# Fewer, larger store packets in a batch-norm + ReLU kernel, and five rows computed in two parts

## Chip, cores, metric

One NeuronCore of one Trainium2 chip. The metric is device time in microseconds (us) of one execution; lower is better. A ratio is the mean time of one kernel's fast runs over that of the kernel before in the same rounds, so not quite the ratio of the medians beside it. Runs of one batch share a chip.

## The reference

```python
# x: (32, 128, 32, 32) float32; one scale and one bias per channel
normalized = (x - running_mean[None, :, None, None]) / np.sqrt(running_var[None, :, None, None] + eps)
scaled = normalized * gamma[None, :, None, None] + beta[None, :, None, None]
return np.maximum(scaled, 0).astype(np.float32)
```

16.78 MB are read and 16.78 MB are written. Each element needs one multiply, one add and one maximum, which ScalarE (ACT) does in a single activation (128 x 1024 elements in 1.227 us on average, 30 of them in the kernel before).

## The kernel before

Each of the 128 partitions holds 16 whole images ("rows" of 1024 floats, 4 KB) of each half of the batch; in DRAM those 16 rows are contiguous. So a DMA of n rows is one run of n x 4 KB per partition. Loads are issued from SyncE, stores from ScalarE after the activations of their rows.

```python
J = 16
TILES = ((0, 0, 2), (0, 2, 4), (0, 4, 8), (0, 8, 16), (1, 0, 16))   # (half, first row, end)
LOAD_CUTS = {(1, 8)}
STORE_CUTS = {(0, 1)}
HALVES = {(0, 0), (0, 1)}          # rows whose activation is done in two parts
...
    for t, a, b in TILES:
        xt = data.tile([P, b - a, HW], F32, name=f"x{t}_{a}")
        cuts = [a] + [j for j in range(a + 1, b) if (t, j) in LOAD_CUTS] + [b]
        for c, d in zip(cuts, cuts[1:]):
            nc.sync.dma_start(out=xt[:, c - a : d - a, :], in_=xr[t, :, c:d, :])
...
        for t, a, b, xt in tiles:
            first = a
            for j in range(a, b):
                step = HW // 2 if (t, j) in HALVES else HW
                for w in range(0, HW, step):
                    nc.scalar.activation(out=xt[:, j - a, w : w + step], in_=xt[:, j - a, w : w + step],
                        func=ACTF.Relu, bias=bias_t[:, j : j + 1], scale=scale_t[:, j : j + 1])
                if j + 1 == b or (t, j + 1) in STORE_CUTS:
                    nc.scalar.dma_start(out=outr[t, :, first : j + 1, :], in_=xt[:, first - a : j + 1 - a, :])
                    first = j + 1
```

The cut parts are the views, the pools, and the parameters (four loads of 0.5 KB, a small matmul that spreads them over the partitions, five small instructions for scale and bias).

## Time and profile before

| | |
|---|---|
| time | 83.92 us, median of 3 (83.75 to 83.99) |
| span in the profile, from first to last instruction | 82.0 us |
| ScalarE busy | 39.1 us |
| loads, bytes per partition's run | 8, 8, 16, 32, 32, 32 KB |
| stores, bytes per partition's run | 4, 4, 8, 16, 32, 64 KB |

This profile is read from the bytes: loads and stores take 48.7% + 47.6% of the 16 DMA engines' span. The lines are in the prediction.

### The profile page before, as it was taken

The numbers are of one execution on the slowest core, as the hardware profiler recorded it, in microseconds if no ns is written. First come the engines' busy times: TensorE is split into PE (matmuls) and PEld (weight loads), VectorE is DVE, ScalarE is ACT, GpSimd is POOL, SyncE is SP. The second block draws the span as 40 slices with busy tenths as digits, with TensorE's granted clock in tenths as the row PEclk, the third lists the DMA queues.
The fourth block names the chain that finished last, engine by engine and source line by source line (L and its number), as shares of the span: only waits on it lengthen the run. The fifth ranks groups of instructions, "written<-read, shape, count | busy, mean of one in ns | idle before, by whom it ended". The sixth has DMA issues, their size and how long they took to land.

```text
span 82.0 us, 120 instructions
## 1 busy us (share of the span) xinstructions
PE 0.7 (1%) x2; PEld 0.5 (1%) x2; DVE 0.8 (1%) x5; ACT 39.1 (48%) x36; POOL 0.8 (1%) x6
## 2 busy tenths in 40 slices
PE   0002000000000000000000000000000000000000
PEld 0002000000000000000000000000000000000000
DVE  0000300000000000000000000000000000000000
ACT  0600477799239999199994199993000000000000
POOL 3000000000000000000000000000000000000000
DMA  2899997979899989999799799998992999996590
GB/s 48 336 424 456 416 544 336 524 322 526 338 434 430 506 358 506 390 434 444 320 460 500 316 424 448 512 432 368 480 736 128 416 512 512 512 512 288 224 512 0
DMA packets 1792, 33.56 MB, mean 409 GB/s; under 512 B 256, under 2 KB 256, under 8 KB 512
## 3 DMA queue, kind: packets, MB, share of 16 engines
q1 hardware_dynamic: 864, 16.78, 48.7%
q10 hardware_dynamic: 928, 16.78, 47.6%
HBM read 16.78 MB, written 16.78 MB: 409 GB/s over the span
## 4 chain that ended last, share of the span: by engine, by line
DMA 56%; ACT 10%; issue 2%; SPq 0%
DMA x<-in_x_dram 56%; ACT x L102 10%; SPq L56 0%
## 5 line engine op out<-in xcount | busy, mean ns | idle before, releaser
L102 ACT ACTIVATE x<-x,bias_t,scale_t 128x1024 f32<-128x1024 f32 (+1 forms) x34 | 37.5, 1177 | 9.9 <-DMA x<-in_x_dram 7.6
L86 ACT ACT_TABLE_LOAD x1 | 1.3, 1283 | 2.6 <-issue 2.6
L86 ACT ACTIVATE std_t<-cols,eps_t 128x16 f32<-128x16 f32 x1 | 0.3, 273 | 4.5 <-PE cols L78 4.5
L78 PE MATMUL cols<-raw,rep 8*128 8x64 f32 x2 | 0.7, 429 | 7.6 <-DMA raw<-in_beta_dram 7.6
L78 PEld LDWEIGHTS cols<-raw,rep 8*128 8x128 f32 x2 | 0.5, 306 | 7.6 <-issue 7.6
L68 POOL TENSOR_SCALAR_AFFINE_SELECT rep<-rep 8x128 f32<-8x128 f32 x1 | 0.4, 392 | 0.1
L88 DVE RECIPROCAL rstd_t<-std_t 128x16 f32<-128x16 f32 x1 | 0.3, 254 | 7.7 <-ACT std_t L86 7.7
L67 POOL MEMSET rep<- 8x128 f32 x1 | 0.2, 194 | 0.3 <-POOLq L130 0.3
L90 DVE TENSOR_TENSOR scale_t<-cols,rstd_t 128x16 f32<-128x16 f32 x1 | 0.2, 175 | 0.1
L92 DVE TENSOR_TENSOR ms_t<-cols,scale_t 128x16 f32<-128x16 f32 x1 | 0.2, 175 | 0.0
L94 DVE TENSOR_TENSOR bias_t<-cols,ms_t 128x16 f32<-128x16 f32 x1 | 0.2, 174 | 0.0
L130 POOL MEMSET const-bfloat16-1.0<- 128x1 bf16 x1 | 0.1, 106 | 0.0
L130 POOL MEMSET const-uint8-127<- 128x1 uint8 x1 | 0.1, 106 | 0.0
L130 POOL MEMSET const-float32-0.0<- 128x1 f32 x1 | 0.1, 103 | 0.3 <-issue 0.3
L130 POOL MEMSET const-float32-1.0<- 128x1 f32 x1 | 0.1, 103 | 0.0
L65 DVE MEMSET eps_t<- 128x1 f32 x1 | 0.1, 59 | 0.9 <-PEq L130 0.9
## 6 DMA issues: line engine op xcount, KB each, us to landing
x<-in_x_dram SPq DMA_DIRECT2D x3, 4096.0 KB, 38.7
out_dram<-x ACTq DMA_DIRECT2D x1, 4096.0 KB, 28.7
x<-in_x_dram SPq DMA_DIRECT2D x2, 1024.0 KB, 5.8
x<-in_x_dram SPq DMA_DIRECT2D x1, 2048.0 KB, 11.3
out_dram<-x ACTq DMA_DIRECT2D x1, 2048.0 KB
out_dram<-x ACTq DMA_DIRECT2D x2, 512.0 KB, 19.6
out_dram<-x ACTq DMA_DIRECT2D x1, 1024.0 KB
raw<-in_running_var_dram ACTq DMA_DIRECT2D x1, 0.5 KB
```

The source lines that it names most:

```text
L65: nc.vector.memset(eps_t, float(eps))
L67: nc.gpsimd.memset(rep, 1.0)
L68: nc.gpsimd.affine_select(out=rep, in_=rep, compare_op=mybir.AluOpType.is_equal, fill=0.0, base=0, pattern=[[0, P // Q], [-1, Q]], channel ...
L78: nc.tensor.matmul(cols.rearrange("p k j -> p (k j)"), rep.rearrange("q r s -> q (r s)"), raw.rearrange("q k j -> q (k j)"), start=True, s ...
L86: nc.scalar.activation(out=std_t, in_=cols[:, 0, :], func=ACTF.Sqrt, bias=eps_t[:, 0:1], scale=1.0)
L88: nc.vector.reciprocal(out=rstd_t, in_=std_t)
L90: nc.vector.tensor_mul(out=scale_t, in0=cols[:, 1, :], in1=rstd_t)
L92: nc.vector.tensor_mul(out=ms_t, in0=cols[:, 2, :], in1=scale_t)
L94: nc.vector.tensor_sub(out=bias_t, in0=cols[:, 3, :], in1=ms_t)
L102: nc.scalar.activation(out=xt[:, j - a, w : w + step], in_=xt[:, j - a, w : w + step], func=ACTF.Relu, bias=bias_t[:, j : j + 1], scale=sc ...
L130: nc = _bacc.Bacc("TRN2", target_bir_lowering=False, num_devices=1)
```

## The change

The intent: one store fewer (packets of 4, 12, 16, 32 and 64 KB), rows 0 to 3 in one tile, and five rows rather than two computed in two parts.

```diff
-TILES = ((0, 0, 2), (0, 2, 4), (0, 4, 8), (0, 8, 16), (1, 0, 16))
+TILES = ((0, 0, 4), (0, 4, 8), (0, 8, 16), (1, 0, 16))

-LOAD_CUTS = {(1, 8)}
+LOAD_CUTS = {(0, 2), (1, 8)}
 STORE_CUTS = {(0, 1)}

-HALVES = {(0, 0), (0, 1)}
+HALVES = {(0, 0), (0, 1), (0, 2), (0, 3), (0, 4)}
```

## The prediction

> **What bounds the kernel now.** I read the page first: its span, its busy row for the DMA engines and its list of queues.
>
> ```profile
> span 82.0 us, 120 instructions
> ...
> PE 0.7 (1%) x2; PEld 0.5 (1%) x2; DVE 0.8 (1%) x5; ACT 39.1 (48%) x36; POOL 0.8 (1%) x6
> ...
> DMA packets 1792, 33.56 MB, mean 409 GB/s; under 512 B 256, under 2 KB 256, under 8 KB 512
> ...
> q1 hardware_dynamic: 864, 16.78, 48.7%
> q10 hardware_dynamic: 928, 16.78, 47.6%
> ```
>
> The two DMA queues, q1 for the loads and q10 for the stores, take 48.7% + 47.6% = 96.3% of what 16 engines have in the span. ScalarE (ACT), the one engine with real work, is busy for less than half of it. The bytes are fixed: 16.78 MB in, 16.78 MB out. The packet count tells the packet's form: 864 is 6 loads x (128 + 16), so each partition's run is one packet, however long, and each DMA has 16 small packets more (4 bytes, its completion signal, one for each engine). So "2 rows" means an 8 KB packet and "16 rows" a 64 KB one.
>
> Next the packet records of the trace, which give start, duration and size of each. A data packet takes 0.159 us for 4 KB, 0.309 for 8 KB, 0.611 for 16 KB, 1.213 for 32 KB and 2.418 for 64 KB; load and store packets of one size take the same, and 16 engines at 32 KB in 1.213 us move 432 GB/s. The first packet starts at 1.75 us, the last ends at 80.81. All durations together are 1263.9 us, or 78.99 us for each of 16 engines, in a stretch of 79.06 us. Summed by whole microseconds, the share is 1.00 to 1.02 in every one from 3 to 79. So the engines never stand empty, and the time is the sum of the packets, plus 1.75 us ahead of them and 1.2 us after.
>
> Then the timeline and the chain of waits, for what stands just behind this bound. Columns of the timeline: start, duration, engine, work.
>
> ```profile
> 9.61 1.52 ACT L102 ACTIVATE x<-x,bias_t,scale_t 128x512 f32<-128x512 f32 x2 [1.02 <-DVE bias_t L94]
> 11.16 0.37 ACTq L110 DMA_DIRECT2D out_dram<-x  x1
> 11.58 1.52 ACT L102 ACTIVATE x<-x,bias_t,scale_t 128x512 f32<-128x512 f32 x2 [0.45 <-ACT x L102]
> 13.13 0.37 ACTq L110 DMA_DIRECT2D out_dram<-x  x1
> 13.55 2.37 ACT L102 ACTIVATE x<-x,bias_t,scale_t 128x1024 f32<-128x1024 f32 x2 [0.45 <-ACT x L102]
> 15.95 0.34 ACTq L110 DMA_DIRECT2D out_dram<-x  x1
> ...
> 34.85 9.16 ACT L102 ACTIVATE x<-x,bias_t,scale_t 128x1024 f32<-128x1024 f32 x8 [1.78 <-DMA x<-in_x_dram]
> 46.87 9.16 ACT L102 ACTIVATE x<-x,bias_t,scale_t 128x1024 f32<-128x1024 f32 x8 [2.86 <-DMA x<-in_x_dram]
> 56.05 0.34 ACTq L110 DMA_DIRECT2D out_dram<-x  x1
> ```
>
> ```profile
> 8.12 38.72 DMA x<-in_x_dram
> 46.84 0.03 issue
> 46.87 0.04 ACT x L102
> 46.91 1.10 issue
> 48.01 8.01 ACT x L102 x7
> ```
>
> The last load lands at 46.84, ACT needs 9.18 us for its eight rows, and the store of the second half, 8 packets of 64 KB on each engine, is issued at 56.05. Its packets start only at 60.98 to 61.49, engine by engine, because the stores of the first half run until then. That is the spare time of the kernel: with its issue of 0.34 us and 0.62 us to a first packet (first load: issue over at 1.18, first packet at 1.80) the last store could start at 57.0, so 4.0 us on the earliest engine are in hand. That number decides this case.
>
> [...] from about 15 us on, an engine alternates a 32 KB load packet and one store packet, and the 4-byte signals take turns of their own. [...]
>
> ```profile
> L102 ACT ACTIVATE x<-x,bias_t,scale_t 128x1024 f32<-128x1024 f32 x30 | 34.5, 1227 | 8.5 <-DMA x<-in_x_dram 7.6 <-ACT x L102 0.9
> L102 ACT ACTIVATE x<-x,bias_t,scale_t 128x512 f32<-128x512 f32 x4 | 3.0, 805 | 1.5 <-DVE bias_t L94 1.0 <-ACT x L102 0.5
> ```
>
> **The change part by part.**
>
> 1. Packets. The loads keep their sizes (the cut at row 2 replaces the border of two tiles). Of the stores, row 1 (8 packets of 4 KB an engine) and rows 2 to 3 (8 of 8 KB) become rows 1 to 3 (8 of 12 KB). A 12 KB packet has no row yet; from 0.159 and 0.309 a further 4 KB costs 0.150, so 0.309 + 0.151 = 0.460 us, an estimate. Each engine sheds 8 x (0.159 + 0.309 - 0.460) = 0.064 us and one signal of under 0.01: **-0.07 us** on the path that sets the end.
>
> 2. Activations. Rows 2, 3 and 4 go from one part to two, 1.52 us a row for about 1.15: +0.37 each. The store issue between rows 1 and 2 goes, with its gap of 0.45 us. Row 1 still starts at 11.58; rows 1 to 3 take 6 x 0.76 = 4.57, so their store is issued at 16.2 (now: rows 2 to 3 at 15.95). Rows 4 to 7 are done at 21.7 instead of 21.0. ACT is then idle until a load lands at 23.9: these delays end there. Nor do the queues notice: row 0's 8 packets, one turn each beside a 32 KB load, last from 14.6 to about 25, so rows 1 to 3 are not wanted before. **0.0 us.**
>
> 3. Shares of the engines. This is what really changes. As long as loads last, one store packet passes for each load packet, so a longer store packet takes time from the loads. First store packets come after 2 or 3 of the 24 load packets of 32 KB; counting signals as turns, store turns 1 to 9 are row 0, 10 to 18 the second store, and from 19 on the third. On the engine that finishes its load last (last data ends at 46.17) 6 packets of the third store pass before the load's signal. Second store: 8 x (0.460 - 0.159) = 2.41 us. Third store, 16 KB for 8 KB: 6 x (0.611 - 0.309) = 1.81. The last load lands 4.2 us later, at 51.1; ACT ends and the last store is issued at 56.05 + 4.2 = 60.3. No bytes are lost by this: the stores have got ahead by as much as the loads are behind.
>
> 4. The end. With 0.34 + 0.62 us the last store can start at about 61.2. The engines run dry of first-half stores at 60.98 - 0.07 = 60.9 to 61.4. The spare 4.0 us are thus spent almost to the nanosecond: an idle gap of 0.3 us on the earliest engine, none on the latest. The engine that ends last sets the time, and it has none if its packets come in time. But the first load's first packets spread over 1.80 to 2.28 us across the engines; a spread of 0.5 would put the last start at 61.7 and up to 0.8 us of gap on an early engine, which ends 61.7 + 19.35 = 81.1 instead of 80.8. So +0.0 to +0.3, taken as **+0.15 us**.
>
> Sum: -0.07 + 0.0 + 0.15 = +0.08; 83.92 + 0.08 = 84.0 us.
>
> **The rivals.** (a) Pure gain: fewer packets, the gap fully hidden: 83.85. For it: equal bytes, and engines that drain late anyway. Against: the margin is about nil. (b) A new wait: the last store comes late for all engines. Should a store's first packet need 1 us more than that of the first load, or ACT start later after the load, then all of it shows: 84.5 to 85. For it: row 0's store was issued at 11.16 and its first packet came at 14.6[...]. (c) ACT becomes the bound by the three extra parts: it would need 1.1 us more on the path, so 85; against it, ACT's idle time before 23.91. (d) Larger store packets spread memory traffic better and run faster: 83; against it, packets of a size take one time in either direction, alone or mixed, at the rate of step 1.
>
> **Range and chances.** Case (a) less run noise of 0.1 gives 83.7 below; (b) in its mild form gives 84.6 above. Faster by 2% would be 82.2, which the packet sum forbids: 1%. Slower by 2% is 85.6, a gap of 1.8 us: 2%. Within: 97%.
>
> **What would show it.** Right: 1648 packets in all (1792 - 144), the last load landing near 51 us, the last store issued near 60.3, a DMA row without a hole or with one under 0.5 us about 61, store of rows 1 to 3 issued near 16.2. Wrong: the last load still at 47 (then turns are not by packet, or 12 KB is cut up); a hole of 1 us or more (then the start of a store is slower than that of the first load); packet durations that differ from those above.

## The result, and the profile after

83.93 us, median of 6 (83.84 to 83.98), against 83.84 for the kernel before in the same rounds (83.53 to 83.99, 6 runs); ratio 1.0016, 95% interval 0.9995 to 1.0038: the same. Measured once more in a later batch, on chip 15 (the run `after_again` below; the record does not name the chip of the first measurement): 84.17 against 83.64, ratio 1.0065 (1.0048 to 1.0082): still the same at 2%, but slower clear of noise.

The page of the changed kernel, same lines as before:

```profile
span 82.2 us, 120 instructions
...
PE 0.7 (1%) x2; PEld 0.5 (1%) x2; DVE 0.8 (1%) x5; ACT 39.8 (48%) x39; POOL 0.8 (1%) x6
...
DMA packets 1648, 33.56 MB, mean 408 GB/s; under 512 B 240, under 2 KB 240, under 8 KB 368
...
q1 hardware_dynamic: 864, 16.78, 48.7%
q10 hardware_dynamic: 784, 16.78, 47.4%
```

144 packets have gone, all of the store queue, whose share fell from 47.6% to 47.4%. The timeline (start, duration, engine, work):

```profile
11.41 0.38 ACTq L110 DMA_DIRECT2D out_dram<-x  x1
11.84 4.33 ACT L102 ACTIVATE x<-x,bias_t,scale_t 128x512 f32<-128x512 f32 x6 [0.46 <-ACT x L102]
16.20 0.37 ACTq L110 DMA_DIRECT2D out_dram<-x  x1
16.62 4.91 ACT L102 ACTIVATE x<-x,bias_t,scale_t 128x512 f32<-128x512 f32 x5 [0.45 <-ACT x L102]
21.56 0.34 ACTq L110 DMA_DIRECT2D out_dram<-x  x1
23.67 9.16 ACT L102 ACTIVATE x<-x,bias_t,scale_t 128x1024 f32<-128x1024 f32 x8 [2.14 <-DMA x<-in_x_dram]
...
51.15 9.16 ACT L102 ACTIVATE x<-x,bias_t,scale_t 128x1024 f32<-128x1024 f32 x8 [5.06 <-DMA x<-in_x_dram]
60.34 0.34 ACTq L110 DMA_DIRECT2D out_dram<-x  x1
```

The price of the larger packets: the last eight rows start at 51.15 in place of 46.87, so the last store is issued at 60.34 in place of 56.05, 4.3 us later. The time hardly moves, since the stores are ahead by what the loads are behind.

The packet records of the trace (start, duration and size of every packet) show how near the end comes to a hole. Times in us; where two are given they are the first and the last of the 16 engines:

| | before | changed | changed, second profile |
|---|---|---|---|
| row 0's store issued | 11.16 | 11.41 | 11.20 |
| engines whose first store packet came after only 2 load packets of 32 KB (the others: 3) | 7 | 0 | 9 |
| second store, packet size and last end | 4 KB, 35.67 | 12 KB, 38.65 | 12 KB, 38.55 |
| third store, packet size and last end | 8 KB, 46.94 | 16 KB, 51.98 | 16 KB, 52.16 |
| last load's completion signal, last engine | 46.48 | 50.76 | 51.46 |
| last store issued | 56.05 | 60.34 | 61.05 |
| engines dry of first-half stores | 60.97 to 61.48 | 61.30 to 61.66 | 61.31 to 61.84 |
| first packet of the last store | 60.98 to 61.49 | 61.31 to 61.67 | 61.89 to 62.04 |
| hole between, mean of 16 | 0.00 | 0.00 | 0.34 |
| all packets, sum for one engine | 78.99 | 79.05 | 79.36 |
| last packet ends | 80.81 | 80.99 | 81.45 |

The records name no engine; a packet is taken to follow the one that ends as it starts. 12 KB packets took 0.460 us. In the first profile the last store's packets start in the very moment the engines become free; in the second they are late.

### The profile page after: what moved, and what is told of

Read it like the earlier page. It is cut to its first block, busy times and chain, and to the rows that moved or that the text cites. A ratio compares the mean times of both kernels' runs of the same rounds, so it can differ in the third digit from the quotient of the medians.

```text
span 82.2 us, 120 instructions
## 1 busy us (share of the span) xinstructions
PE 0.7 (1%) x2; PEld 0.5 (1%) x2; DVE 0.8 (1%) x5; ACT 39.8 (48%) x39; POOL 0.8 (1%) x6
## 2 busy tenths in 40 slices
DMA packets 1648, 33.56 MB, mean 408 GB/s; under 512 B 240, under 2 KB 240, under 8 KB 368
## 3 DMA queue, kind: packets, MB, share of 16 engines
q10 hardware_dynamic: 784, 16.78, 47.4%
## 4 chain that ended last, share of the span: by engine, by line
DMA 60%; ACT 11%; ACTq 1%; issue 0%
DMA x<-in_x_dram 53%; ACT x L102 11%; DMA raw<-in_beta_dram 7%; ACTq L63 1%
## 5 line engine op out<-in xcount | busy, mean ns | idle before, releaser
L102 ACT ACTIVATE x<-x,bias_t,scale_t 128x1024 f32<-128x1024 f32 (+1 forms) x37 | 38.2, 1111 | 13.2 <-DMA x<-in_x_dram 11.3
```

## The experiments

The theory to test: on an engine one store packet passes for each load packet (between 16 and 46 us 332 load and 339 store packets of data start in the kernel before, 296 and 292 in the changed one); larger early stores push the last load back; ScalarE and the last store follow it; and this shows in the time only as far as the last store's first packet comes after the engines have run dry. The rivals: bytes alone count; the queues share by bytes; the split rows, or a packet size in itself, cost or save time. All results were correct.

| run | median (runs) | before | ratio (95%) | last rows start | last store issued | mean hole |
|---|---|---|---|---|---|---|
| `store24` | 86.50 (4) | 83.86 | 1.0315 (1.0282 to 1.0348) | 54.18 | 63.37 | 2.31 |
| `store48` | 93.08 (4) | 83.86 | 1.1105 (1.1058 to 1.1151) | 60.05 | 69.24 | 8.82 |
| `store48_lastcut` | 84.32 (4) | 83.86 | 1.0073 (1.0023 to 1.0123) | 59.99 | 69.17 | see text |
| `tiles_only` | 84.52 (4) | 83.86 | 1.0082 (1.0054 to 1.0111) | 51.58 | 60.77 | 0.23 |
| `halves_only` | 83.80 (4) | 83.50 | 1.0048 (1.0019 to 1.0076) | 46.93 | 56.12 | 0.00 |
| `all64` | 83.67 (6) | 83.50 | 1.0020 (1.0002 to 1.0038) | see text | 60.25 | 0.52, at 41 |
| `after_again` | 84.17 (6) | 83.64 | 1.0065 (1.0048 to 1.0082) | 51.86 | 61.05 | 0.34 |
| `tiles_only_again` | 84.42 (6) | 83.64 | 1.0090 (1.0073 to 1.0106) | 51.45 | 60.63 | 0.26 |
| `row0_whole` | 84.24 (6) | 83.64 | 1.0070 (1.0056 to 1.0085) | 51.60 | 60.79 | 0.32 |
| `row0_quarters` | 84.06 (5) | 83.64 | 1.0047 (1.0033 to 1.0061) | 51.13 | 60.32 | 0.00 |
| `big` | 87.41 (6, five slow) | 83.50 | none | 55.18 | 64.36 | 3.25 |
| `big_held` | 87.33 (6, five slow) | 83.52 | none | 54.80 | 63.99 | 2.91 |

### Larger third store: `store24`, `store48`

```diff
-TILES = ((0, 0, 4), (0, 4, 8), (0, 8, 16), (1, 0, 16))
-LOAD_CUTS = {(0, 2), (1, 8)}
+TILES = ((0, 0, 4), (0, 4, 16), (1, 0, 16))
+LOAD_CUTS = {(0, 2), (0, 8), (1, 8)}       # the loads stay as they are
-STORE_CUTS = {(0, 1)}
+STORE_CUTS = {(0, 1), (0, 10)}             # store24; store48 keeps {(0, 1)}
```

> Stores with packets of 4, 12, 24, 24 and 64 KB: the third store is 1.5 times as large as in the changed kernel, nothing else moves. Theory (an engine passes one store packet for each load packet, and the changed kernel has no spare time left before its last store): 6 packets of the third store pass before the last load's signal, each 0.912 us (estimate) in place of 0.611, so the last load lands 1.8 us later than 51.15, at 52.9 to 53.0; the last store is issued near 62.1, and its first packet comes 0.97 us after that, near 63.1; the engines have been dry since 61.3 to 61.7, a hole of 1.4 to 1.8 us, and the time is 85.4 to 85.8. Rival 1 (bytes are all that counts, the order is hidden): 83.9. Rival 2 (the queues share by bytes, not by packets): the last load lands at 51 still, and 83.9.

> Stores with packets of 4, 12, 48 and 64 KB. Theory: 6 packets of 1.815 us (estimate) in place of 0.611 pass before the last load's signal, so it lands 7.2 us later than 51.15, at 58.4; the last store is issued near 67.6, its first packet near 68.5, the hole is 6.9 to 7.2 us, and the time 90.8 to 91.2 although the bytes are the same and there are 144 packets fewer than in the changed kernel. Both rivals: 83.9.

Both rivals fall: the bytes are the same, `store48` has 144 packets fewer than the changed kernel, and it takes 9 us more. The theory has the direction and most of the size; it was short by about 1 us in `store24` and 2 us in `store48`. The cause is a count. In the changed kernel's first profile every engine let 3 load packets of 32 KB pass before its first store packet, and 6 packets of the third store went ahead of the last load's completion signal. In `store48` all 16 engines let only 2 pass (in `store24` 11 of 16), and then 7 go ahead, the seventh between the last data packet and the signal, which is a packet with a turn of its own (4 bytes, 0.009 us in the traces before and after). That is not the doing of the larger store: where row 0's store comes in was settled before the third store was issued (see `row0_whole` below). With 7: 7 x 1.815 - 6 x 0.611 = 9.04 us for `store48`, measured 60.05 - 51.15 = 8.90; and 7 x 0.912 - 6 x 0.611 = 2.72 for `store24`, measured 54.18 - 51.15 = 3.03, of which some 0.3 to 0.4 us are load packets that took longer than in the changed kernel (mean 1.260 against 1.245 us, 24 to an engine).

### Filling the hole: `store48_lastcut`

```diff
-STORE_CUTS = {(0, 1)}
+STORE_CUTS = {(0, 1), (1, 8)}              # on top of store48
```

> As store48, and the store of the second half cut in two at row 8 (packets of 32 and 32 KB). Theory: the last load lands at 58.4 as in store48, but rows 0 to 7 of the second half have been stored from about 46 on the queue and fill the hole: they give each engine 8 x 1.213 = 9.7 us of work from 61.5 to 71.2, and the very last store is issued near 67.6. No hole; 83.9 plus 8 packets of 0.008 us = 84.0. A rival for store48's loss, that 48 KB packets are slow by themselves, expects 90 to 91 here too.

ScalarE's timeline is that of `store48`. First `store48`, then `store48_lastcut`:

```profile
60.05 9.16 ACT L102 ACTIVATE x<-x,bias_t,scale_t 128x1024 f32<-128x1024 f32 x8 [13.68 <-DMA x<-in_x_dram]
69.24 0.34 ACTq L110 DMA_DIRECT2D out_dram<-x  x1
```

```profile
46.32 0.34 ACTq L110 DMA_DIRECT2D out_dram<-x  x1
59.99 9.16 ACT L102 ACTIVATE x<-x,bias_t,scale_t 128x1024 f32<-128x1024 f32 x8 [13.70 <-DMA x<-in_x_dram]
69.17 0.34 ACTq L110 DMA_DIRECT2D out_dram<-x  x1
```

And the stretch from 62 to 70 us in each (the last two columns are the DMA engines' share and GB/s; a packet counts where it starts, so a share can pass 1):

```profile
62.00:70.00 8.00, 0.00 (x0) 0.00 (x0) 0.00 (x0) 7.21 (x7) 0.00 (x0) 1.00 0.00 0
```

```profile
62.00:70.00 8.00, 0.00 (x0) 0.00 (x0) 0.00 (x0) 7.14 (x7) 0.00 (x0) 1.00 1.06 459
```

Both have ScalarE busy to the end of these 8 us and the last store issued at 69.2. One has nothing for the engines to do meanwhile, the other has the first part of the last store: 93.08 against 84.32 us. So 48 KB packets are not slow by themselves; the loss is the empty engines. The 84.32 are still 0.3 us above the 84.0 expected. The profile is of the slowest of the four runs (84.99): no engine stands empty in it (0.01 us on average), but two of the 16, with a load packet of about 2.2 us each, end at 82.0, the others by 80.8.

### Taking the change apart: `tiles_only`, `halves_only`

```diff
-HALVES = {(0, 0), (0, 1), (0, 2), (0, 3), (0, 4)}
+HALVES = {(0, 0), (0, 1)}                                        # tiles_only: on the changed kernel
```

```diff
-HALVES = {(0, 0), (0, 1)}
+HALVES = {(0, 0), (0, 1), (0, 2), (0, 3), (0, 4)}                # halves_only: on the kernel before
```

> The change without its three more split rows (only rows 0 and 1 in two parts). Theory: the activations of rows 2 to 4 are 1.1 us shorter in sum and all of that lies before ScalarE's wait for the load that lands at 23.7, so the last load, the last store and the time stay: 51.1, 60.3 and 83.9 us. A rival (the split rows cost ScalarE time on the path): 83.0 or less.

> The kernel before with rows 2, 3 and 4 also in two parts, stores as before. Theory: the three extra parts cost ScalarE 1.1 us, all of it ahead of its wait for the load that lands at 23.9; the last load still lands near 46.8, the last store is issued near 56.1 and its packets start near 61: 83.8 to 83.9 us. Rival (they are on the path): 84.9.

Within the span the split rows do nothing: in `halves_only` the last rows start at 46.93, the last store is issued at 56.12, and the last packet ends at 80.72 (before: 46.87, 56.05, 80.81). Yet its median is 0.3 us above that of before, and `tiles_only`, where nothing should have come, took 84.52. Part of `tiles_only` is the theory once more: on one single engine the first store came in after 2 load packets, and that engine's load signal came at 51.18, the other fifteen's at 50.39 to 50.70. The last rows started 0.40 us after the latest of them, at 51.58 (in the kernel before, the changed one and `after_again` 0.39 to 0.40). The rest is outside the span; that is taken up below.

### One chip, four kernels: `after_again`, `tiles_only_again`, `row0_whole`, `row0_quarters`

The last two move the issue of row 0's store, and so the place at which it comes in among the load packets:

```diff
-HALVES = {(0, 0), (0, 1), (0, 2), (0, 3), (0, 4)}
+HALVES = {(0, 1), (0, 2), (0, 3), (0, 4)}                        # row0_whole
```

```diff
-                step = HW // 2 if (t, j) in HALVES else HW
+                step = HW // 4 if (t, j) == (0, 0) else HW // 2 if (t, j) in HALVES else HW   # row0_quarters
```

> The changed kernel again, on the chip of the next three. Theory: 83.9, ratio to before 1.000 to 1.003 if its first stores come in after 3 load packets of 32 KB, as in its first profile; 84.2 to 84.4 if they come in after 2.

> The change without its three more split rows, beside the changed kernel on one chip. Theory A (the three split rows do nothing; what tiles_only lost before was the place at which its first store came in, after 2 load packets on half of its engines): it equals after_again within 0.2 us when both have the same place, and the trace shows after how many load packets the first stores start. Theory B (the split rows themselves are worth time): 84.5 again against 83.9 with the same place of the first store.

> The changed kernel with row 0 in one part: its store is issued 0.37 us sooner, near 11.0. Theory A: it comes in after 2 load packets on every engine, so 7 rather than 6 packets of the third store pass before the last load's signal, which lands 0.6 us later, near 51.7; last store issued near 60.9, first packet 0.85 later at 61.8, engines dry at 61.3 to 61.7: hole up to 0.5, time 84.2 to 84.4. Sooner is slower. Theory B: 83.9 or a little less, since rows are ready sooner.

> The changed kernel with row 0 in four parts: its store is issued 0.45 us later, near 11.9. Theory A: after 3 load packets on every engine, 6 packets of the third store, last load lands at 51.1 or sooner, no hole: 83.8 to 83.9, the lowest of these four though ScalarE works longer. Theory B: 83.9 to 84.4, as rows are ready later.

The issue of row 0's store and the chain's end in the changed kernel on this chip, to be set beside 11.41, 51.15 and 60.34 of the first profile:

```profile
11.20 0.37 ACTq L110 DMA_DIRECT2D out_dram<-x  x1
...
51.86 9.16 ACT L102 ACTIVATE x<-x,bias_t,scale_t 128x1024 f32<-128x1024 f32 x8 [5.46 <-DMA x<-in_x_dram]
61.05 0.34 ACTq L110 DMA_DIRECT2D out_dram<-x  x1
```

The first stores came in after 2 load packets on 9 of 16 engines in `after_again`, on 15 in `tiles_only_again`, on all 16 in `row0_whole` and on none in `row0_quarters`. (In `tiles_only` it was one engine, not the half that the expectation above says.) The holes follow: 0.34, 0.26, 0.32 and 0.00 us.

Over all profiled runs that store row 0 on its own the count goes by the moment at which row 0's store was issued: at 10.77 to 11.06 us (four runs) 15 or 16 engines let only 2 load packets pass, at 11.12 to 11.20 (four runs) 7 to 14, at 11.39 to 11.62 (three runs) one or none. One and the same kernel falls on either side, because the parameters land a few tenths sooner or later from execution to execution (the last of them at 7.73 and 7.53 us in the changed kernel's two profiles): the changed kernel issued at 11.41 and 11.20, `tiles_only` at 11.39 and 11.05.

`row0_whole` has its row ready 0.85 us before `row0_quarters` (store issued at 10.77 against 11.62) and is 0.18 us slower, 84.20 to 84.35 against 84.03 to 84.11: sooner is slower, as theory A had it. But `row0_quarters` missed its 83.8 to 83.9 by 0.2 us, `row0_whole` met its 84.2 to 84.4 only with the same 0.2 us, and `tiles_only_again` is 0.25 us above `after_again` although the median span of the six runs is 82.45 us in both.

That leftover lies outside the span. Device time less span, of the profiled run of each kernel:

| less span | kernels |
|---|---|
| 1.70 to 1.72 us | before, changed, `after_again`, `store24`, `store48_lastcut`, `all64`, `big`, `big_held` |
| 1.88 to 1.96 us | `halves_only`, `tiles_only`, `tiles_only_again`, `row0_whole`, `row0_quarters`, `store48` |

Two levels, 0.2 us apart, and a kernel that was measured twice has the same one twice. The other runs agree: with the record's spans, which have one decimal, every run of the first line lies at 1.66 to 1.77 and every run of the second at 1.85 to 2.01. What sets it is open: it is before the first or after the last instruction of the program. It accounts for most of `halves_only`'s 0.3 us, for `row0_quarters`' miss and for `tiles_only_again` against `after_again`. The changed kernel and the one before are on the same level, so their comparison is not touched.

### Fewest packets: `all64`, `big`, `big_held`

```diff
-TILES = ((0, 0, 4), (0, 4, 8), (0, 8, 16), (1, 0, 16))
+TILES = ((0, 0, 16), (1, 0, 16))
-LOAD_CUTS = {(0, 2), (1, 8)}
+LOAD_CUTS = set()                          # all64; big and big_held: {(0, 8), (1, 8)}
-STORE_CUTS = {(0, 1)}
-HALVES = {(0, 0), (0, 1), (0, 2), (0, 3), (0, 4)}
+STORE_CUTS = set()
+HALVES = set()
```

`big` and `big_held` also move the first half's store in the program to after row 3 and row 7 of the second half.

> Two loads and two stores, all of 64 KB packets, no row in two parts. The sum of packets is the smallest possible here, 32 x 2.418 = 77.38 us, 0.6 less than before. But both stores come just in time at best: first half landed at about 21.9, computed at 40.2, its store's first packet near 41.2, when the loads end at 40.7 to 41.4; second half computed near 59.9, its first packet near 60.9, when the first store ends near 60.5. Theory: holes of 0 to 0.5 us twice, time 83.2 to 84.0. A time above 84.5 would say that ScalarE waits longer than worked out.

> Four loads of 32 KB packets and two stores of 64 KB packets, the first store held back until row 3 of the second half is computed so that the loads keep ahead; no row in two parts. Theory (the time is the sum of the packets on an engine, each about 0.0084 us beyond its bytes, plus a fixed head and tail): nominal sum 32 x 1.213 + 16 x 2.418 = 77.50 us against 77.96 for the kernel before (both without signals), so 0.45 to 0.5 us less: 83.3 to 83.5, ratio to before about 0.995. If the start-up stretch of the first packets is smaller with larger first packets, 0.2 us less again. Rival (a fixed cost per DMA rather than per packet, or no cost at all): 83.8.

> As big (four loads of 32 KB packets, two stores of 64 KB), with the first store's instruction moved from after row 3 to after row 7 of the second half. In big it was issued at 33.05, four rows sooner than its place in the program, and ran into five load packets. Theory: [...] the store is issued near 37.6, its packets come in near 39 to 40 beside one or two last load packets on each engine, the last load lands by 46.5, the last store is issued by 56 and waits its turn until 60: no hole, and the sum of packets is 0.45 to 0.5 us less than in before. Time 83.0 to 83.4, ratio 0.994 to 0.997. If the time is 83.8 with no hole in the trace, packets' own cost is not what the time is made of.

The 37.6 is `big`'s issue at 33.05, four rows ahead of its place, put off by four rows of 1.145 us (an eighth of the 9.16 us that the timelines show for eight); it was an estimate.

`all64`: the packets sum to 78.31 us an engine, 0.68 less than before, near the 0.6 expected. But the engines ran dry at 41.17 to 41.62 and the first store came at 41.86 to 42.00, a hole of 0.52; at the end there was none. What the packets gave, the hole took: 83.67 against 83.50.

`big` failed as a test. Its store was to wait for row 3 of the second half; it was issued at 33.05, and each engine's last three or four load packets and the load's signal then took turns with 64 KB packets of 2.4 us, which made a hole of 3 us at the end. `big_held`, with the store behind row 7, did the same:

```profile
14.90 19.33 ACT L104 ACTIVATE x<-x,bias_t,scale_t 128x1024 f32<-128x1024 f32 x17 [1.02 <-DVE bias_t L96]
33.14 0.38 ACTq L112 DMA_DIRECT2D out_dram<-x  x1
34.14 8.01 ACT L104 ACTIVATE x<-x,bias_t,scale_t 128x1024 f32<-128x1024 f32 x7
54.80 9.16 ACT L104 ACTIVATE x<-x,bias_t,scale_t 128x1024 f32<-128x1024 f32 x8 [12.65 <-DMA x<-in_x_dram]
```

24 activations stand ahead of this store in the program, and it was issued when 16 were done: eight ahead of its place. Why it could go ahead of them is not shown. The sixteenth activation, the last of the 16 rows that are stored, ended at 33.11 and the store was issued at 33.14; in `big`, where 20 activations stand ahead of it, it was issued at 33.05. So a place later by four rows moved the issue by 0.09 us, and both fit a wait for the 16 rows alone. Five of the six runs of each were over 1.5% above their fastest (85.61 and 85.77) and so are counted as slow; both profiles, with their holes, are of such runs. Even the fastest are above every run of before. Whether a version with few packets and no hole gains the 0.5 us of its packets stays untried.

These kernels also show what a queue's turn means for a tiny transfer. The parameters' last landing and the first work after it, in the changed kernel (loads begin with 8 KB packets), `big_held` (32 KB) and `all64` (64 KB):

```profile
2.08 5.65 DMA raw<-in_beta_dram
```

```profile
2.10 10.68 DMA raw<-in_beta_dram
```

```profile
20.37 0.65 PE L78 MATMUL cols<-raw,rep 8*128 8x64 f32 x2 [20.37 <-DMA raw<-in_beta_dram]
```

From their last issue, 0.5 KB land after 5.65, 10.68 and about 18 us. The packet records show the turns. The first parameter's packet and signal went through at 1.76 us, ahead of the loads; the packets and signals of the other three first start at 5.97, 7.18, 8.40, 9.62, 10.83 and 12.05 us in `big_held`, one load packet of 1.213 us apart, and at 7.33, 9.75, 12.17, 14.59, 17.01 and 19.43 in `all64`, one of 2.418 us apart.

## Why the prediction was right, point by point

- **The sum.** 84.0 predicted, 83.93 measured: its closeness is partly luck, since two terms missed in opposite directions, the packets (+0.06 us in place of -0.07) and the hole (none in place of 0.15).
- **What bounds the kernel.** Right. The engines were full from start to end in both kernels (their share from 2 to 80 us is 1.01 in both, the mean hole 0.00), and what moved the time by more than a few tenths were holes: 0.3 us of hole cost some tenths, 8.82 us cost 9.2. The prediction's "the time is the sum of the packets, plus 1.75 us ahead of them and 1.2 us after" gives the span, 82.0; the device time is 1.7 us more.
- **Step 1, packets, -0.07.** The packet's duration was right to the nanosecond (0.460), the count too (1648). The gain didn't arrive: the sum for an engine rose, by 0.06 us in the first profile and 0.37 in the second, mostly because some load packets of 32 KB took up to 1.6 us (mean 1.245 in the changed kernel's first profile, 1.233 before, so 0.3 us over 24 packets). In that profile the 14 that took over 1.5 us all start between 25.7 and 26.0 us, the last load packet before the second store's first packet (27.19). What stretches them was not found.
- **Step 2, activations, 0.0.** Right that it costs nothing: stores at 16.20 and 21.56 (16.2 and 21.7 predicted), then ScalarE still waits 2.14 us for the load. The 16.20 itself is luck: row 1 started at 11.84, not 11.58, and the six half rows took 4.33 us, not 4.57. And `halves_only` moves nothing within the span.
- **Step 3, shares of the engines.** Right: last rows at 51.15 (51.1), last store issued at 60.34 (60.3). `store24` and `store48` bear it out: with 24 and 48 KB in place of 16 the last rows start at 54.18 and 60.05. What the step took as fixed, 6 packets of the third store, is 6 or 7, by whether the first store comes in after 3 or 2 load packets; the engine with the larger count decides. The step misread this count in the kernel before: after the last engine's load signal at 46.48 only one 8 KB packet is left, which ends at 46.79, so 7 had passed. With 7 before and 6 after, its sum is 2.41 + 6 x 0.611 - 7 x 0.309 = 3.91 us, and the signal moved by 4.28; most of the rest is the stretched load packets. So meeting 4.2 is partly luck. With 7 and 7, as in the second profile, the sum is 4.52, and the signal moved by 4.98.
- **Step 4, the end, +0.15.** The size of the hole was right (nil to some tenths), the term only as a mean of two cases that the step did not separate: no hole in the first profile, 0.34 us in the second. Which one comes goes by the issue of row 0's store, 11.41 or 11.20 us; that the first measurement had none was luck. The first packet of a store on an empty queue came 0.84 to 0.88 us after its issue began, rather than 0.96 (0.50 us after the issue's end in `after_again` and `all64`, where the first load's 0.62 was expected), and on all 16 engines within 0.15 us rather than 0.5; in the first profile that was just enough.
- **The rivals.** (a) has the hidden gap of the first measurement but not its gain. A mild (b) fits the second (84.17; 84.5 was its lower end), with another cause than the two that it names: a seventh packet. (c) falls by `halves_only`. (d) falls: packets of a size took the same time, or longer (32 KB stores 1.213 us before and after, loads 1.233 and 1.245 on average).

Open are what stretches the load packets, the 0.2 us outside the span, and how much of the second measurement's 0.53 us is hole: the profiled run has 0.34, but it was the slowest of its six, and the kernel before was not profiled on that chip. After a hole the 64 KB packets also took 2.428 us on average in place of 2.418, 0.08 us for the eight of an engine.

## What to carry to other kernels

In these kernels two DMA queues shared full engines, one packet was one partition's run, and about as many store packets as load packets went through while both had work (339 and 332 before, 292 and 296 after the change, between 16 and 46 us). So the run lengths decided which queue got ahead: 24 or 48 KB packets of the third store in place of 16 moved the start of the last rows from 51.15 to 54.18 and 60.05 us, and the last store with it. That was free until the last store's first packet fell behind the engines' last work, and then it cost about microsecond for microsecond (holes of 2.31 and 8.82 us put the last packet's end off by 2.77 and 8.63); so in such a case work out that margin before the change, and leave more than one packet of it (0.611 us here, since the count of packets ahead varied by one), or cut the last store so that its first part can fill the hole (84.32 us in place of 93.08). A store placed four or eight activations behind the last row it stores was not held back by them: it was issued at 33.05 and 33.14, in `big_held` 0.03 us after that row.
